# Eleven modulation units move from the context's chain into the first block's chain

## The chip, the cores and the metric

The kernel runs on one core of a Trainium2 chip. The metric is the device time of one execution in microseconds (us); several runs are given by their median. A core has a matrix engine (PE, with PEld as its weight loads), a vector engine (DVE), a scalar engine (ACT), a general engine (POOL) and a sync engine (SP), each with an instruction stream of its own, and 16 transfer engines (DMA) that move data between the chip's memory and the core's buffers. Here all large loads are issued from SP, in one order.

## The reference

Two networks follow each other on 256 tokens of width 1024. The first is one block: gated attention in two branches, a cross attention, and a mixture of 32 experts of which every token uses two. The second has two layers on the tokens `h` and on a context `hc` of 256 rows. Both streams are modulated by vectors that come from `c` and `c_ctx`:

```
def first_block(x, ...):
    merged = (sigmoid(gate_a) * (y_a @ w_branch_a) + sigmoid(gate_b) * (y_b @ w_branch_b))
    x = x + merged @ w_out
    x = x + cross_attention(rms_norm(x), rms_norm(mem), w_cq, w_ckv, w_co)
    return x + hier_moe(rms_norm(x), ..., w_exp_gate, w_exp_up, w_exp_down)

def second_block(x, c, ctx, c_ctx, ...):
    for layer in range(2):
        mod  = (silu(c)     @ ada_w[layer] + ada_b[layer])   # 9 vectors of 1024
        modc = (silu(c_ctx) @ ada_w[layer] + ada_b[layer])
        h  = h  + 0.5 * mod[2]  * swiglu(modulate(h,  mod[0],  mod[1]),  ...)
        hc = hc + 0.5 * modc[2] * swiglu(modulate(hc, modc[0], modc[1]), ...)
        yx, yc = mixer(modulate(h, mod[3], mod[4]), modulate(hc, modc[3], modc[4]))
        h = h + mod[5] * yx
        h = h + 0.5 * mod[8] * swiglu(modulate(h, mod[6], mod[7]), ...)
        # the same for hc, in the first layer
```

A modulation unit, in what follows, is one of the nine vectors of one layer, for both streams at once: a product of two columns with a 1024 x 1024 part of `ada_w`, which is 4 MB. There are eighteen. The context's chain through the second network needs nothing of the first: it needs `ctx`, the modulation and the weights alone.

## The kernel before

The program is written as two streams, each a `Stream` with its own buffers. **fore** (tiles whose names begin with f) runs the first network (`first_block`, `moe`) and then the tokens of the second network (`tokens()`). **back** (names with b) runs the context's chain (`context()`). Loads of fore are 1 MB and go through a ring of four buffers (`raw`, shown as fraw); those of back are 0.5 MB, with a ring of five (braw). Every instruction of a stream follows the one before it on the same engine (`Kern.link`), so a stream's order is the order in which it is written. Between the two streams a scheduler chooses by priorities: `SEG` gives each part of the program a start and a slope, and the priority grows with the matmul work that the stream has issued. The first block and the routing start at -5000, so they come first where they can, and back fills in; the expert part starts at 365, among the context's parts c0a (300), c0b (530), c0c (680).

A weight that is loaded is split into a high and a low part (ACT writes sph, DVE for fore and POOL for back write spl), and each product is three matmuls of 128x256. Two kinds of load are used without a split: the experts' weights (in_w_eg, in_w_eu, in_w_ed; 128x512 matmuls on 32 columns of weights) and `ada_w` (128x256 matmuls against the two columns of `scol`, written into fps or bps).

The stages in time are these. The first block: projections, attention, then eight passes of gates (`branch_gates(n)` with two loads' worth of w_g and half a load of w_br), four passes of the output projection (`out_proj`), a query projection, the cross attention, and the routing. Then the expert loads, in eight groups of 24 loads of 1 MB (16 up and gate, 8 down). Then a loop for further blocks of the routing, which has no pass here; it splits the program, and everything of `context()` must stand ahead of it. Last the tokens, with the rest of the context's work (`late`, by the table `PLAN`: 'r' is a step of the context's third feed-forward part, 'a' a modulation unit, 'k' keys and values for the odd mixer).

The modulation units before: twelve at the head of `context()` (all nine of layer 0, three of layer 1), by `Kern.ada` in loads of 0.5 MB that take turns in the tags raw, k4, xh and xl of back; two in the token stage ('aa' in `PLAN[8]`); four in the odd mixer, by `ada_wide`. `ada_close` ends each with a transpose and an addition on DVE. The first feed-forward part of the context (c0a) needs units 0 to 2 of layer 0, its even mixer (c0b) units 3 to 5, and so on.

Of the kernel before, what the change touches and what calls it, by code (L numbers as in the profile page):

```python
# [20 lines left out]
KC = 8  # L21
# [9 lines left out]
ADA_TAGS = ('raw', 'k4', 'raw', 'xh', 'k4', 'raw', 'xl', 'k4', 'raw')  # L31
# [71 lines left out]
class Ahead:  # L103
# [7 lines left out]
    def step(self, c):  # L111
        K, S, nc = self.K, self.S, self.K.nc
        if self.X is None:
            xh, xl = (S.t(tag, [128, KC, T + 2], F32R) for tag in ("xh", "xl"))
            s = self.shift[:, :, None].to_broadcast([128, KC, 2])
            nc.scalar.activation(xh[:, :, T:], s, AF.Copy)
            nc.vector.tensor_tensor(xl[:, :, T:], s, xh[:, :, T:].bitcast(F32), op=OP.subtract)
            self.X = X2([xh[:, k] for k in range(KC)], [xl[:, k] for k in range(KC)])
        K.split_to(self.X.h[c][:, :T], self.X.l[c][:, :T], self.res[c], self.g[:, c:c + 1])
# [29 lines left out]
class Kern:  # L149
# [209 lines left out]
    def out_proj(self, S, src, X, res, gate, step=None):  # L359

        nc = self.nc
        for u in range(4):
            raw = self.pair(S, src[u])
            p = S.ps([128, 2, T])
            for i in range(2):
                self.proj_f(S, raw[i], KC, X, p[:, i])
            if gate is None:
                nc.vector.tensor_tensor(res[:, 2 * u:2 * u + 2], res[:, 2 * u:2 * u + 2], p, op=OP.add)
            else:
                self.update(res, p, gate, 2 * u)  # L370
            if step:
                step(2 * u)
                step(2 * u + 1)
            self.squares(S, res, 2 * u)

    def update(self, res, p, gate, d):
# [173 lines left out]
    def ada_wide(self, S, l, ms):  # L550

        for m in ms:
            p = S.ps([128, 512])
            for u in range(KC // 2):
                raw = self.load(S, self.I["ada_w"][l, m, u])
                for i in range(2):
                    k = 2 * u + i
                    mv = raw[:, i * 1024:(i + 1) * 1024].rearrange("p (c j i) -> p j c i", j=4, i=32)
                    for j in range(4):
                        self.mm(p[32 * j:32 * j + 32, 0:256], self.sc[:, k], mv[:, j], k == 0, k == KC - 1)  # L560
                if u < KC // 2 - 1:
                    yield
            self.ada_close(S, l, m, p)
            yield

    def ada_close(self, S, l, m, p):
        nc = self.nc
# [142 lines left out]
    def first_block(self, S):  # L710
# [66 lines left out]
        p = S.ps([128, 512])  # L777
# [9 lines left out]
        raw = self.pair(S, I["w_ck"])  # L787
        p = S.ps([128, 2, T])
# [87 lines left out]
        for i in range(8):  # L876
# [7 lines left out]
            if i < 6:  # L884
                p = queries(i + 2)
# [15 lines left out]
        def branch_gates(n):  # L901
            p = S.ps([128, 2, T])
            ts = []
            raw = self.pair(S, I["w_g"][n])
            for s in range(2):
                self.proj_f(S, raw[s], KC, X, p[:, s])
            for s in range(2):
                t = S.t("k1", [128, T])
                nc.scalar.activation(t, p[:, s], AF.Tanh, scale=0.5)
                ts.append(t)  # L910
            return ts
# [10 lines left out]
        XB = X2([ybh[:, i] for i in range(4)], [ybl[:, i] for i in range(4)])  # L922
        mg = [S.t("k4", [128, 4, T]) for _ in range(2)]
        for n in range(8):
            ts = ahead if n == 0 else branch_gates(n)
            if n % 2 == 0:
                rb = self.load(S, I["w_br"][n // 2])
            p = S.ps([128, 2, T])
            o = (n % 2) * 1024
            self.proj_f(S, rb[:, o:o + 512], 4, XA, p[:, 0])  # L930
            self.proj_f(S, rb[:, o + 512:o + 1024], 4, XB, p[:, 1])
            for s in range(2):
                nc.vector.scalar_tensor_tensor(ts[s], ts[s], 1.0, p[:, s], op0=OP.add, op1=OP.mult)
            nc.vector.tensor_tensor(mg[n // 4][:, n % 4], ts[0], ts[1], op=OP.add)
# [7 lines left out]
        raw = self.pair(S, I["w_cq"])  # L942
        q = S.t("k2", [128, 2, T])
        p = S.ps([128, 2, T])
        for n in range(2):
            self.proj_f(S, raw[n], KC, X, p[:, n])
        nc.scalar.activation(q, p, AF.Copy, scale=0.125)
        rx = self.rstd_cols(S, self.stats(S, chunks))
        yy = S.t("k4", [128, 2, 2, T], F32R)
        ps = {}  # L950

# [8 lines left out]
        for c in range(2):  # L960
            Ps, r = self.softmax(S, pp[2 * c:2 * c + 2], (T, T), rx)
            for s in range(2):
                self.scaled(Ps[s], r[:, s], (T, T))
                ps[c, s] = Ps[s]
        for c in range(2):
            PT = S.t("k4", [128, 2, 2, T])
            for s in range(2):
                pt = S.ps([128, 2, 2, 128])
                for b in range(2):
                    for kb in range(2):  # L970
                        nc.tensor.transpose(pt[:, kb, b], ps[c, s][:, b, kb * 128:(kb + 1) * 128], ident)
                if s == 0:
                    nc.vector.tensor_copy(PT[:, s], pt.rearrange("p k b q -> p k (b q)"))
                else:
                    nc.scalar.activation(PT[:, s], pt.rearrange("p k b q -> p k (b q)"), AF.Copy)
            po = S.ps([128, 512])
            for kb in range(2):
                for s, rows in enumerate(HALVES):
                    hv = slice(64 * (2 * c + s), 64 * (2 * c + s) + 64)
                    self.mm(po[rows, :T], vc[:, kb, hv], PT[:, s, kb, :], kb == 0, kb == 1)  # L980
            self.split_to(yy[:, c, 0], yy[:, c, 1], po[:, :T])
        Y = X2([yy[:, 0, 0], yy[:, 1, 0]], [yy[:, 0, 1], yy[:, 1, 1]])
        raw = self.load(S, I["w_co"])
# [16 lines left out]
    def moe(self, S):  # L1000
# [3 lines left out]
        st = self.stats(S, None)  # L1004
        rx = self.rstd_cols(S, st)
        lg = self.token_major(S, 36, 2, ((self.w_route, keep),))

        xh, xl = S.t("xh", [128, 2, 1024], F32R), S.t("xl", [128, 2, 1024], F32R)
        hm = [(xh[:, b], xl[:, b]) for b in range(2)]

        def turn(b, a):
            pt = S.ps([128, 512])
            for i in range(4):
                nc.tensor.transpose(pt[:, i * 128:(i + 1) * 128], keep[4 * a + i][:, b * 128:(b + 1) * 128],
                                    self.ident)
            self.split_to(hm[b][0][:, a * 512:(a + 1) * 512], hm[b][1][:, a * 512:(a + 1) * 512], pt, rx[:, b:b + 1])
# [4 lines left out]
        def ct(n):  # L1021
            used[0] += n
            return scratch[:, used[0] - n:used[0]]
# [24 lines left out]
        tt(dg, G, gm[:, :, None].to_broadcast([128, 2, 4]), op=OP.subtract)  # L1048
        nc.scalar.activation(dg, dg, AF.Exp)
        turn(0, 0)  # L1050
        gw = S.t("c", [128, 2])
        red(gw, dg, axis=AX.X, op=OP.add)
        nc.vector.reciprocal(gw, gw)
# [10 lines left out]
        tt(e2, t2, t1, op=OP.subtract)  # L1064
        nc.scalar.activation(e2, e2, AF.Exp)
        turn(0, 1)
        ts(r, e2, 1.0, None, op0=OP.add)
        nc.vector.reciprocal(r, r)
        tt(w[:, 0], r, gw, op=OP.mult)
# [12 lines left out]
        self.mm(p[:, 64:96], self.ones, A[:, 1], False, True)  # L1082
        turn(1, 0)
        turn(1, 1)
        cnt, nsp, inc, sb = ct(32), ct(32), ct(32), ct(32)
        rank = ct(64).rearrange("p (b n) -> p b n", b=2)
        nc.vector.tensor_copy(rank, p[:, :64].rearrange("p (b n) -> p b n", b=2))
# [705 lines left out]

SPILL = 4
DEFER = 0
PLAN = {-1: 'rrr', 0: 'r', 6: 'r', 8: 'raak'}
PLAN_N = 32
CUT = ((0, 9, 9, 9, 9), (0, 3, 3, 3, 3))
FORE = dict(raw=4, sph=3, spl=3, xh=1, xl=1, k1=6, k2=4, k4=6, c=16, q1=4, dg=2, ld=1, dst=6, wg=2, gc=5, c72=1, rope=1)
BACK = dict(raw=5, sph=3, spl=3, xh=1, xl=1, k1=4, k2=4, k4=3, c=16, q1=2, wg=1, gc=4, c72=1)  # L1800
SEG = dict(c1b=(1150, 2), first=(-5000, 1), ada=(0, 0), c0a=(300, 1.25), c0b=(530, 1.3), c0c=(680, 1.3), ada1=(950, 3), c1a=(1050, 4.8),
# [4 lines left out]
def kernel(ctx: ExitStack, tc: tile.TileContext, I, out, dbg=None, stop=None):  # L1806
# [7 lines left out]
    def context():  # L1814
        c = K.cres
        back.seg(*SEG["ada"])
        def ada(part):
            for l in range(2):
                ms = range(CUT[l][part], CUT[l][part + 1])
                for _ in K.ada(back, l, ms, ADA_TAGS if part == 0 else ("raw",)):  # L1820
                    pass
        K.adapart = ada
        ada(0)
        back.seg(*SEG["c0a"])
        X = K.modulated(back, c, 0, 0, 1)
        K.ffn(back, c, X, 0, 0, K.mods_col(0, 2, 1))
        if dbg:
            dbg("hc0a", c)
        ada(1)
        back.seg(*SEG["c0b"])  # L1830
        X = K.modulated(back, c, 0, 3, 1)
        K.even(back, c, X, K.mods_col(0, 5, 1), 1)
        if dbg:
            dbg("hc0b", c)
        ada(2)
        back.seg(*SEG["c0c"])
        X = K.modulated(back, c, 0, 6, 1)
        K.ffn(back, c, X, 0, 1, K.mods_col(0, 8, 1))
        ada(3)
        back.seg(*SEG["c1a"])  # L1840
        X = K.modulated(back, c, 1, 0, 1)
        K.c1a = K.ffn_steps(back, c, X, 1, 0, K.mods_col(1, 2, 1))
        K.nada = CUT[1][-1]
        late(PLAN.get(-1, ""))
        if dbg:
            dbg("hc0c", c)
# [50 lines left out]
            dbg("h1c", x)  # L1897

    K.cur, K.stream = back.chain, back
    if stop != "first0":  # L1900
        context()
    K.cur, K.stream = fore.chain, fore
    fore.seg(*SEG["first"])
    K.first_block(fore)
    if stop in ("first", "first0"):
        return
    fore.seg(*SEG["route"])
    K.moe(fore)
    if stop == "moe":
        return  # L1910
    steps = tokens()
# [167 lines left out]
```

## Time and profile before

| what | value |
|---|---|
| median of 3 runs | 2572.41 us (2569.87 to 2574.41) |
| profiled run, its own time | 2570.27 us |
| its span in the profile | 2568.5 us |
| mean granted clock of PE | 0.967 |
| PE busy | 2379.0 us, 93% |
| bytes moved | 617.37 MB |

Durations below come from the profiled run; the span runs from its first to its last recorded instruction. Busy time is a mean over stages with different limits, so the rows are given by stages: the opening (0 to 64 us), two stretches with the modulation's loads (64 to 211), gates, output projection and query (211 to 370), cross attention and routing (370 to 448), the expert loads (448 to 1319) and the tokens. PEclk is the granted clock of PE as a share of full speed; the DMA share is the mean over the core's 16 transfer engines.

### The profile page before, as it was taken

The numbers are of one execution on the slowest core, as the hardware profiler recorded it, in microseconds if no ns is written. First come the engines' busy times: TensorE is split into PE (matmuls) and PEld (weight loads), VectorE is DVE, ScalarE is ACT, GpSimd is POOL, SyncE is SP. The second block draws the span as 40 slices with busy tenths as digits, with TensorE's granted clock in tenths as the row PEclk, the third lists the DMA queues.
The fourth block names the chain that finished last, engine by engine and source line by source line (L and its number), as shares of the span: only waits on it lengthen the run. The fifth ranks groups of instructions, "written<-read, shape, count | busy, mean of one in ns | idle before, by whom it ended". The sixth has DMA issues, their size and how long they took to land. (4 is left out here: it accounts for less than half of the span.)

```text
span 2568.5 us, 48423 instructions
## 1 busy us (share of the span) xinstructions
PE 2379.0 (93%) x19032; PEld 2065.5 (80%) x19032; DVE 1481.0 (58%) x3179; ACT 1186.0 (46%) x2342; POOL 729.7 (28%) x584
## 2 busy tenths in 40 slices
PE   6999998998988999999579999999999899899998
PEld 4767998885666887877259998878999899767998
DVE  6546667325444333252157676657767766677766
ACT  4434554344433433443035555545555555465554
POOL 1001245663425665756041004231000100424000
PEclk9999998999989999999889999999999999899998
DMA  9896543997979997988874554462455455355552
GB/s 376 307 343 252 186 158 115 387 355 287 379 285 358 353 352 297 363 328 334 337 295 174 183 182 139 166 208 106 154 191 181 148 182 186 109 197 197 180 182 99
DMA packets 115238, 617.37 MB, mean 240 GB/s; under 512 B 13232, under 2 KB 14704, under 8 KB 63936
## 3 DMA queue, kind: packets, MB, share of 16 engines
q1 hardware_dynamic: 113616, 610.20, 64.4%
q0 software_dynamic: 1392, 4.06, 0.5%
q8 instruction: 150, 2.46, 0.4%
q14 instruction: 80, 0.66, 0.1%
HBM read 612.11 MB, written 2.10 MB: 239 GB/s over the span
## 5 line engine op out<-in xcount | busy, mean ns | idle before, releaser
L58 POOL TENSOR_TENSOR bspl<-braw,bsph 128x512 fp32r<-128x512 f32 x468 | 608.2, 1308 | 894.7 <-ACT bsph L58 759.2
L58 ACT ACTIVATE fsph<-fraw 128x512 fp32r<-128x512 f32 x764 | 478.5, 628 | 516.7 <-PE fps L58 432.8
L58 DVE TENSOR_TENSOR fspl<-fraw,fsph 128x512 fp32r<-128x512 f32 x712 | 501.1, 707 | 286.2 <-ACT fsph L58 281.2
L58 PE MATMUL fps<-fxh,fspl 128*128 128x256 f32 (+1 forms) x2000 | 572.5, 286 | 5.0 <-POOL fspl L58 2.5
L58 PE MATMUL fps<-fxh,fsph 128*128 128x256 f32 (+1 forms) x2000 | 573.3, 287 | 3.0 <-ACT fxh L58 2.4
L58 PE MATMUL fps<-fxl,fsph 128*128 128x256 f32 (+1 forms) x2000 | 568.6, 284 | 6.4 <-DVE fxl L58 6.4
L58 ACT ACTIVATE bsph<-braw 128x512 fp32r<-128x512 f32 x468 | 291.0, 629 | 394.8 <-PE bps L58 325.4
L58 PEld LDWEIGHTS fps<-fxl,fsph 128*128 128x128 f32 x2000 | 382.3, 191 | 9.8 <-DVE fxl L58 9.1
L58 PEld LDWEIGHTS fps<-fxh,fspl 128*128 128x128 f32 x2000 | 381.2, 191 | 11.1 <-DVE fspl L58 5.3
L58 PEld LDWEIGHTS fps<-fxh,fsph 128*128 128x128 f32 x2000 | 382.7, 191 | 9.2 <-ACT fxh L58 4.1
L58 PE MATMUL bps<-bxh,bsph 128*128 128x256 f32 x1264 | 364.3, 288 | 6.1 <-ACT bsph L58 4.3
L58 PE MATMUL bps<-bxh,bspl 128*128 128x256 f32 x1264 | 364.5, 288 | 3.9 <-POOL bspl L58 3.7
L58 PE MATMUL bps<-bxl,bsph 128*128 128x256 f32 x1264 | 361.3, 286 | 2.6 <-ACT fk L58 2.2
L58 PE MATMUL fps<-fk,fsph 128*128 128x256 f32 x1632 | 298.7, 284 | 1.8 <-ACT fk L58 1.1
L58 PEld LDWEIGHTS bps<-bxh,bsph 128*128 128x128 f32 x1264 | 244.2, 193 | 29.6 <-issue 11.9
L58 PEld LDWEIGHTS bps<-bxh,bspl 128*128 128x128 f32 x1264 | 244.0, 193 | 24.1 <-POOL bspl L58 16.8
L58 PEld LDWEIGHTS fps<-fk,fsph 128*128 128x128 f32 x1632 | 254.8, 192 | 5.6 <-ACT fk L58 2.3
L58 PEld LDWEIGHTS bps<-bxl,bsph 128*128 128x128 f32 x1264 | 244.3, 193 | 10.8 <-issue 8.1
L58 PE MATMUL fps<-fraw,fk 128*32 128x512 f32 (+1 forms) x1600 | 211.6, 643 | 33.2 <-DMA fraw<-in_w_eu_dram 19.9
L58 POOL TENSOR_TENSOR fk<-fk,fk 128x512 f32<-128x512 f32 x16 | 21.2, 1322 | 774.0 <-ACT fk L58 768.9
L58 PE MATMUL fps<-fk,fspl 128*128 128x256 f32 x816 | 230.8, 283 | 0.0
L58 DVE SCALAR_TENSOR_TENSOR bk<-bk,bps 128x256 f32<-128x256 f32 (+1 forms) x148 | 60.4, 412 | 249.1 <-ACT bk L58 247.2
(359 smaller groups left out, 3477.9 us busy)
## 6 DMA issues: line engine op xcount, KB each, us to landing
fraw<-in_ffn_in_dram SPq DMA_DIRECT2D x88, 1024.0 KB, 4.9
braw<-in_ffn_in_dram SPq DMA_DIRECT2D x132, 512.0 KB, 6.5
fraw<-in_w_eg_dram SPq DMA_DIRECT2D x66, 1024.0 KB, 7.3
fraw<-in_w_eu_dram SPq DMA_DIRECT2D x66, 1024.0 KB, 9.2
fraw<-in_w_ed_dram SPq DMA_DIRECT2D x66, 1024.0 KB, 7.1
fraw<-in_ffn_out_dram SPq DMA_DIRECT2D x44, 1024.0 KB, 4.9
braw<-in_ffn_out_dram SPq DMA_DIRECT2D x66, 512.0 KB, 6.3
braw<-in_ada_w_dram SPq DMA_DIRECT2D x59, 512.0 KB, 7.8
```

The lines of the kernel that those rows point to most:

```text
L58: r = f(*args, **kw)
```

## The change

The head of `context()` keeps three units (0 to 2 of layer 0). Eleven others (3 to 8 of layer 0, 0 to 4 of layer 1) are now written into the fore stream, by a generator `ada_mix` that loads two times 1 MB in a step and uses them at once; a unit is two steps. `mixed(place)` runs the steps that the table `MIX` names: one ahead of each of the eight gate passes, one in each of the four output passes, and ten more from the query projection to the ranks of the routing. `context()` is a generator: what follows c0a is recorded inside `moe`, after the last step, since it needs these units. The two units of the token stage are among the eleven, and `PLAN[8]` loses its 'aa'. The four in the odd mixer stay.

```diff
@@ out_proj
                 step(2 * u + 1)
+                self.mixed("out")
@@ Kern
+    def ada_mix(self, S, units):
+        for l, m in units:
+            p = S.ps([128, 512])
+            for u in range(0, KC // 2, 2):
+                raws = [self.load(S, self.I["ada_w"][l, m, u + i]) for i in range(2)]
+                for i in (1, 0):
+                    for a in range(2):
+                        mv = raws[i][:, a * 1024:(a + 1) * 1024].rearrange("p (c j i) -> p j c i", j=4, i=32)
+                        for j in range(4):
+                            self.mm(p[32 * j:32 * j + 32, 0:256], self.sc[:, 2 * (u + i) + a], mv[:, j],
+                                    u == 0 and i == 1 and a == 0, u > 0 and i == 0 and a == 1)
+                if u == 0:
+                    yield
+            self.ada_close(S, l, m, p)
+            yield
+
+    def mixed(self, place):
+        for _ in range(MIX.get(place, 0)):
+            next(self.mix)
@@ first_block
         for n in range(8):
+            self.mixed("gates")
             ts = ahead if n == 0 else branch_gates(n)
...
+        self.mixed("query")
...
         for c in range(2):
+            self.mixed("flip")
@@ moe
         lg = self.token_major(S, 36, 2, ((self.w_route, keep),))
+        self.mixed("route")
...
         turn(0, 0)
+        self.mixed("first")
...
         turn(0, 1)
+        self.mixed("second")
...
         turn(1, 1)
+        self.mixed("rank")
+        assert next(self.mix, None) is None
+        yield
@@
-PLAN = {-1: 'rrr', 0: 'r', 6: 'r', 8: 'raak'}
+PLAN = {-1: 'rrr', 0: 'r', 6: 'r', 8: 'rk'}
-CUT = ((0, 9, 9, 9, 9), (0, 3, 3, 3, 3))
+MIX_UNITS = [(0, m) for m in range(3, 9)] + [(1, m) for m in range(5)]
+MIX = dict(gates=1, out=1, query=2, flip=1, route=1, first=1, second=2, rank=2)
@@ context
-        ada(0)
+        for _ in K.ada(back, 0, range(3), ADA_TAGS):
+            pass
         back.seg(*SEG["c0a"])
...
+        yield
         back.seg(*SEG["c0b"])
...
-        K.nada = CUT[1][-1]
+        K.nada = 5
@@ driver
-        context()
+    ctx_steps = context()
+    next(ctx_steps)
...
+    K.mix = K.ada_mix(fore, MIX_UNITS)
     K.first_block(fore)
...
-    K.moe(fore)
+    moe = K.moe(fore)
+    next(moe)
+    K.cur, K.stream = back.chain, back
+    assert next(ctx_steps, None) is None
+    K.cur, K.stream = fore.chain, fore
+    assert next(moe, None) is None
```

The order on SP around the second load of w_g, before (128x2048 is 1 MB, 128x1024 is 0.5 MB; braw, bk, bxh and bxl are back's buffers):

```order
L58 DMA fraw_10665<-in_w_g_dram 128x2048
L58 DMA bk_620<-in_ada_w_dram 128x1024
L58 DMA braw_630<-in_ada_w_dram 128x1024
L58 DMA bxh_632<-in_ada_w_dram 128x1024
L58 DMA bk_642<-in_ada_w_dram 128x1024
L58 DMA braw_644<-in_ada_w_dram 128x1024
L58 DMA bxl_654<-in_ada_w_dram 128x1024
```

The same place on SP after, in the gates:

```order
L58 DMA fraw_4820<-in_w_g_dram 128x2048
L58 DMA fraw_4890<-in_w_br_dram 128x2048
L58 DMA fraw_4928<-in_ada_w_dram 128x2048
L58 DMA fraw_4930<-in_ada_w_dram 128x2048
L58 DMA braw_1617<-in_ffn_in_dram 128x1024
L58 DMA fraw_4953<-in_w_g_dram 128x2048
L58 DMA fraw_5060<-in_ada_w_dram 128x2048
L58 DMA fraw_5062<-in_ada_w_dram 128x2048
```

The loads of `ada_w` stood one after another in back's several buffers, and the gates' own loads between them; now they alternate with the gates' loads in the one ring fraw, and back's loads there are weights of the context's feed-forward part.

On PE, at the start of a gate pass, before (fps is an accumulator of fore; fxh and fxl are the high and low parts of the block's input):

```order
L58 MATMUL fps_11167<-fk_10603,fsph_11184 128x256
L58 MATMUL fps_11167<-fk_10602,fspl_11185 128x256
L58 MATMUL fps_11203<-fxh_9080,fsph_11206 128x256
L58 MATMUL fps_11203<-fxl_9081,fsph_11206 128x256
L58 MATMUL fps_11203<-fxh_9080,fspl_11207 128x256
```

At the start of such a pass on PE after:

```order
L58 MATMUL fps_5283<-fk_4586,fsph_5300 128x256
L58 MATMUL fps_5283<-fk_4585,fspl_5301 128x256
L58 MATMUL fps_5319<-fraw_5322,scol 32x256 x8
L58 MATMUL fps_5319<-fraw_5320,scol 32x256 x8
L58 MATMUL fps_5340<-fxh_3063,fsph_5343 128x256
L58 MATMUL fps_5340<-fxl_3064,fsph_5343 128x256
L58 MATMUL bps_1512<-bk_1311,bsph_1508 128x256
```

A step of sixteen matmuls on two 1 MB loads stands ahead of the pass, and matmuls of the context's feed-forward part (bps) stand inside it.

On SP near the end of the expert loads, before, the last load of the context's chain stands in the seventh group, among its down weights (in_w_ed):

```order
L58 DMA braw_8796<-in_ffn_out_dram 128x1024
L58 DMA braw_8868<-in_ffn_out_dram 128x1024
L58 DMA braw_8870<-in_ffn_out_dram 128x1024
L58 DMA fraw_13922<-in_w_ed_dram 128x2048
L58 DMA fraw_13924<-in_w_ed_dram 128x2048
L58 DMA fraw_13934<-in_w_ed_dram 128x2048
```

After, it stands ahead of that group's first load:

```order
L58 DMA braw_12029<-in_ffn_out_dram 128x1024
L58 DMA braw_12101<-in_ffn_out_dram 128x1024
L58 DMA braw_12103<-in_ffn_out_dram 128x1024
L58 DMA fraw_13817<-in_w_eg_dram 128x2048
L58 DMA fraw_13819<-in_w_eu_dram 128x2048
L58 DMA fraw_13829<-in_w_eg_dram 128x2048
```

The context's chain ends some sixteen expert loads earlier in the order.

## Rows read from the trace of the kernel before

**Rows 1.** The page's shares: engine, busy us, share of the span, instructions.

```profile
PE 2379.0 (93%) x19032; PEld 2065.5 (80%) x19032; DVE 1481.0 (58%) x3179; ACT 1186.0 (46%) x2342; POOL 729.7 (28%) x584
```

**Rows 2.** Windows: length; busy PE, PEld, DVE, ACT, POOL; PEclk, DMA share, GB/s.

```profile
0.00:64.00 64.00, 41.27 (x323) 29.70 (x323) 43.03 (x134) 29.16 (x62) 7.80 (x18) 0.97 0.98 376
64.00:141.00 77.00, 73.61 (x703) 57.58 (x703) 42.85 (x111) 30.03 (x79) 0.00 (x0) 0.98 0.86 315
141.00:211.00 70.00, 64.00 (x565) 39.70 (x563) 31.69 (x87) 21.43 (x58) 0.00 (x0) 1.00 0.94 357
211.00:370.00 159.00, 154.78 (x1281) 147.72 (x1280) 109.61 (x224) 87.81 (x184) 39.75 (x31) 1.00 0.51 178
370.00:448.00 78.00, 70.89 (x530) 66.49 (x530) 56.67 (x127) 37.19 (x76) 44.74 (x35) 0.91 0.38 123
448.00:552.00 104.00, 104.00 (x864) 85.69 (x860) 31.95 (x61) 41.22 (x75) 68.06 (x54) 1.00 0.97 374
552.00:838.00 286.00, 256.42 (x1866) 188.47 (x1859) 129.08 (x334) 115.50 (x234) 125.34 (x101) 0.93 0.85 326
838.00:1226.00 388.00, 380.10 (x3074) 312.75 (x3073) 140.71 (x274) 154.29 (x287) 245.47 (x190) 0.99 0.90 339
1226.00:1319.00 93.00, 54.07 (x337) 19.52 (x336) 12.15 (x25) 8.81 (x15) 7.55 (x6) 0.82 0.89 334
1319.00:2568.00 1249.00, 1179.90 (x9512) 1117.87 (x9512) 883.22 (x1805) 660.53 (x1277) 190.94 (x152) 0.97 0.48 169
```

**Rows 3.** A window of the token stage in which PE is dense.

```profile
1412.00:1541.00 129.00, 129.00 (x1091) 129.00 (x1091) 90.19 (x168) 67.81 (x122) 0.00 (x0) 1.00 0.52 184
```

**Rows 4.** Groups by shape, whole span: modulation from 1 MB loads (busy, mean ns, idle).

```profile
L58 PE MATMUL fps<-fraw,scol 128*32 128x256 f32 x256 | 17.1, 385 | 0.0
```

**Rows 5.** Window 64 to 211, modulation alone; one of three 512-column groups there.

```profile
64.00:211.00 147.00, 45.91 (x592) 18.24 (x592) 0.00 (x0) 0.99 0.90 335
...
L58 PE MATMUL fps<-fsph,fxh 128*128 128x512 f32 x16 | 6.8, 423 | 0.0
```

**Rows 6.** Waits of PE, 64 to 211 us: total us, times, longest.

```profile
PE fps L58 <- DVE fq L58: 3.8, 3, 2.1
PE fps L58 <- DVE fk L58: 2.5, 1, 2.5
...
PE fps L58 <- ACT fq L58: 1.3, 1, 1.3
```

**Rows 7.** The window with expert loads and no filler (30 loads).

```profile
1226.00:1307.00 81.00, 44.77 (x264) 10.63 (x263) 7.92 (x18) 3.20 (x6) 0.03 (x1) 0.79 0.93 355
```

**Rows 8.** Waits of PE, 1226 to 1319 us.

```profile
PE fps L58 <- DMA fraw<-in_w_eu_dram: 19.9, 7, 4.5
PE fps L58 <- DMA fraw<-in_w_ed_dram: 12.2, 4, 4.9
```

**Rows 9.** Timeline of PE: the first expert matmuls, of four loads (start, duration).

```profile
447.58 3.64 PE L58 MATMUL fps<-fraw,fk 128*32 128x512 f32 x32
```

**Rows 10.** Waits of PE, 552 to 838 us, the two largest.

```profile
PE bps L58 <- DVE bk L58: 13.8, 10, 2.9
PE bps L58 <- ACT bk L58: 11.7, 10, 3.0
```

**Rows 11.** Waits of SP's queue, 448 to 1226 us, the largest.

```profile
SPq L58 <- POOL bspl L58: 369.3, 132, 10.2
```

**Rows 12.** Token stage: PE's wait in 1641 to 1740 us; two windows of it.

```profile
PE bps L58 <- DMA braw<-in_ada_w_dram: 6.1, 2, 3.4
...
1701.00:1717.00 16.00, 16.00 (x144) 12.20 (x136) 6.37 (x17) 7.22 (x14) 0.56 (x1) 1.00 0.84 268
1717.00:1733.00 16.00, 9.95 (x97) 6.49 (x86) 7.03 (x15) 3.46 (x7) 3.46 (x3) 0.79 0.84 288
```

**Rows 13.** Transfer issues on SP: count, KB each, median us from issue to landing.

```profile
fraw<-in_ada_w_dram SPq DMA_DIRECT2D x16, 1024.0 KB, 4.9
fraw<-in_w_g_dram SPq DMA_DIRECT2D x8, 1024.0 KB, 4.9
```

More of the change, by code (lines that the diff above doesn't have):

```diff
@@ L1816, in context @@
         back.seg(*SEG["ada"])
[L1817 to L1822, printed above, removed]
-        ada(0)
+        for _ in K.ada(back, 0, range(3), ADA_TAGS):
+            pass
         back.seg(*SEG["c0a"])
@@ L1828, in context @@
             dbg("hc0a", c)
-        ada(1)
+        yield
         back.seg(*SEG["c0b"])
@@ L1834, in context @@
             dbg("hc0b", c)
-        ada(2)
         back.seg(*SEG["c0c"])
@@ L1838, in context @@
         K.ffn(back, c, X, 0, 1, K.mods_col(0, 8, 1))
-        ada(3)
         back.seg(*SEG["c1a"])
@@ L1899 @@
     K.cur, K.stream = back.chain, back
-    if stop != "first0":
-        context()
+    ctx_steps = context()
+    next(ctx_steps)
     K.cur, K.stream = fore.chain, fore
     fore.seg(*SEG["first"])
+    K.mix = K.ada_mix(fore, MIX_UNITS)
     K.first_block(fore)
```

## Prediction

> **What bounds the kernel now.** I read the shares of the page first [rows 1]: the matrix engine (PE) is busy for 2379 of 2568.5 us. So the whole run is nearly a sum of PE work, and a change that only moves PE work can win or lose only in the 190 us in which PE stands idle, or where it is slowed. The windows by stage [rows 2] show where those are. The opening (0 to 64 us) has loads at 0.98 of the transfer engines. From 64 to 211 us the modulation loads run at 0.86 and 0.94. From 211 to 448 us (gates, output projection, query, routing) PE is nearly full and the transfer engines are at 0.51 and 0.38. From 448 to 1319 us run the expert loads, at 0.85 to 0.97, with the context's matmuls as filler beside them; this ends in a stretch without filler (1226 to 1319 us) in which PE is busy for 54 of 93 us at a granted clock of 0.82. The rest, 1249 us, is the token stage, PE-bound. The first expert matmul stands at 447.58 us [rows 9].
>
> So two stretches are short of transfer time (64 to 211, and 448 to 1319), one lies between them that has it to spare, and the end of the expert stage is short of PE work. The change takes modulation loads out of the first and puts them into the spare stretch. But the context's other work comes forward with it.
>
> **Stage 1, up to the first expert matmul.** The orders show what stands ahead of that matmul on PE. Context matmuls of 256 columns: 713 before, 1431 after, so 718 more, since the chain has no longer twelve units to wait for but three. One costs 0.118 us where PE is dense (1091 instructions in 129 us, [rows 3]): 718 × 0.118 = **+85 us**, on the path, as PE is what sets this stage. Modulation units ahead of it: 12 before, 14 after, the two extra ones from the token stage. The four units that the token stage runs from 1 MB loads take 17.1 us in 256 instructions [rows 4], 4.3 us each: **+8.6 us**.
>
> What is won: from 64 to 211 us PE's own work comes to 592 modulation instructions × 0.067 (17.1 us ÷ 256) = 39.7 us, 48 instructions of 512 columns (three rows of 16, of which one stands in [rows 5]; 0.23 us each beside two of 256) = 11 us, and the other 628 of the 1268 × 0.118 = 74 us: 125 of 147 us. So 22 us are lost there, while loads run near full. After, 36 MB of the modulation's loads have left this stretch. Waits for the block's own vector work stay: 3.8 + 2.5 + 1.3 us [rows 6]. I take **−15 us**, between −22 (all of it) and −8.
>
> What is paid: the 22 steps fetch 44 loads of 1 MB through the fore stream's ring of four, in turn with w_g, w_br and w_out, and a load lands 4.9 us after its issue [rows 13]. In the SP queue after, two of the gates' eight passes need 2 w_g, 1 w_br and 4 modulation loads and about 1 MB of the context's: 8 MB beside some 25 us of PE work (17.0 + 4.3 + about 3.5 us, counted as above), 320 GB/s. The row from 448 to 552 us moves 374 GB/s [rows 2], so the rate suffices; what may not suffice is the distance by which the ring of four runs ahead. Counted in the orders at the prices above, a fore load in gates and output projection had 17 to 40 us of PE work between its issue and its use before; it has 7 to 14 us after. The nearest row is the expert stage from 838 to 1226 us: the same ring of four, 339 GB/s, and PE idle for 7.9 of 388 us. For about 220 us of such steps that makes 4.5 us; with the vector engines' splits in between I double it: **+9 us**, from 0 to +60. The upper end is each step showing one landing less its matmuls, 22 × (4.9 − 2.15).
>
> Routing (370 to 448 us) has 7.1 idle us [rows 2], with steps and context matmuls now queued in it; 0 to −5, taken as 0. The six extra ada_close on the fore chain are two vector instructions each at places where PE works on; nothing. Stage 1: 447.6 + 85 + 8.6 − 15 + 9 = **535 us**.
>
> **Stage 2, the expert loads, 447.6 to 1319.3 us (871.7 us).** What came forward is missing here: 718 matmuls. In the orders the context's last chained matmul stands ahead of expert load 146 of 192 now, ahead of load 162 before; so 46 loads instead of 30 run with no filler. In the trace the 30 took 81 us (1226 to 1307), 2.7 us each, at 355 GB/s and a granted clock of 0.79 [rows 7], with PE waiting for up and down weights 19.9 + 12.2 us in the 93 us [rows 8]. Sixteen more at 2.8 us: the stretch grows from 93 to **138 us**.
>
> The part with filler (448 to 1226 us, 778 us) loses 85 us of filler, and 16 loads' own PE work (3.64 us for 4 loads [rows 9], 14.6 us): if PE sets it, 778 − 99 = 679. If transfers set it: bytes issued between the routing's list and the end of the stage fall from 292.6 to 276.9 MB in the orders; less 1 MB for each load without filler, 262.6 and 230.9 MB, and at the rate of before (262.6 MB in 778 us, 337 GB/s) 684 us. Both rules agree, because both engines were nearly full; I take **678**. Against a faster one stands the context's even mixer: from 552 to 838 us PE waits for its vector work (13.8 + 11.7 us, [rows 10]) and no row there names a transfer; that chain stays whole and only moves earlier, into groups 0 to 2. On SP the largest wait is for the context's splits on POOL (369 us, [rows 11]), and both streams' loads queue behind it; it keeps. Stage 2: 678 + 138 = **816 us**, 56 less.
>
> **Stage 3, the tokens, 1249 us.** Two units leave: 2 × 4.3 = 8.6 us of PE; the two waits for their loads, 6.1 us, and 16 us at a granted clock of 0.79 around them [rows 12] leave too: −8.6 to −22, taken **−14**. What was late behind them is the context's next step, which now stands a little earlier.
>
> **The sum.** 535 + 816 + 1235 = 2586 us against 2568.5; with the 1.8 us by which the profiled run lies above its span, 2588. That run is 2.1 us under the median of 2572.41, so half of that is added: **2589 us**, 0.7% slower. In one sentence: the change wins about 15 us where loads were short and 14 us among the tokens, and pays some 31 us more than it gains for moving filler from the expert loads, which leave PE idle, to the first block, which doesn't.
>
> **Rivals.** *(A) Transfers set the expert stage, and fewer bytes and less PE work end it earlier: faster.* For it: transfer shares of 0.97, 0.85 and 0.90 [rows 2], and a stretch at 374 GB/s where PE was full too. PE's own work with filler is 778 − 38 idle = 740, less 99 = 641 us; the tail 46 × 2.7 = 124: at the very best 765 us. With +72 in stage 1 and −20 in stage 3 that would be 2515. Half of the way there from my own sum, with stage 1 at +78, stage 2 at 790 (−82) and stage 3 at −16: 2570 + 78 − 82 − 16 = **2550 us**. Against it: the waits in 552 to 838 us are not for transfers. It decides if the part with filler runs at 355 GB/s or more instead of 337.
>
> The Trainium skill's page "DMA: Bandwidth & Descriptors" (Specifications) gives about 358 GB/s as the limit of one core; by it the 276.9 MB would need 773 us at least, and the best of (A) would be 2523 us. The 374 GB/s of the row are above that figure, so by this trace it is no limit, and no number here uses it.
>
> *(B) The ring of four shows its loads at most steps: clearly slower.* Three quarters of the upper end above, +45 us instead of +9, and nothing given back later, as the token stage starts when the expert stage ends: 2589 + 36 = **2625 us**. For it: two consecutive 1 MB loads per step, in the only ring that w_g also uses, and a lookahead of 7 us at the shortest against 4.9 us to landing plus a split. Against it: the same ring feeds the experts with hardly a wait.
>
> *(C) It cancels.* The stage that loses its filler is helped by as much as stage 1 pays (stage 2 at 800 instead of 816): **2573 us**, within 0.2%.
>
> **How the numbers follow.** My forecast, slower by 6 to 40 us, has 0.45; (A) 0.25; (B) 0.15; (C) 0.15. About 5 us, 0.2%, is what a measurement of this kernel can tell from no change. Faster 0.25, same 0.15, slower 0.60. The range takes in most of (A) and of (B): 2542 to 2632 us; the forecast's own is 2578 to 2612.
>
> **What would show it.** The first expert matmul at 525 to 550 us; at 560 or more (B) is right, and PE's waits between 211 us and it will name modulation or w_g loads. The stretch 64 to 211 us with hardly a modulation load and PE full. The expert stage 800 to 830 us long with PE waiting for expert loads over its last 46; under 790, with over 350 GB/s ahead of that stretch, (A). The token stage 1227 to 1241 us. The forecast fails if the context's extra matmuls stand ahead of the first expert matmul in gaps that PE had anyway, since the 85 us are priced as dense work.

## The result, and the profile after

The changed kernel takes 2588.69 us (median of 7 runs, 2583.34 to 2592.09), the kernel before 2573.78 us beside it: a ratio of 1.0057, with a 95% interval of 1.0044 to 1.0069. It is slower by 15 us. Its profiled run has a span of 2586.9 us, 18.4 more than that of before.

The windows by stage of the changed kernel (columns as in [rows 2]; the stages begin at the same places of the program: opening, attention, gates to query, cross attention and routing, expert loads with filler, expert loads without, tokens):

```profile
0.00:64.40 64.40, 41.78 (x322) 30.07 (x323) 42.96 (x133) 29.03 (x61) 7.80 (x18) 0.97 0.97 373
64.40:144.50 80.10, 77.84 (x642) 69.23 (x641) 55.09 (x140) 44.75 (x111) 15.23 (x12) 0.96 0.46 160
144.50:228.20 83.70, 83.27 (x645) 78.42 (x643) 50.45 (x105) 44.80 (x101) 44.85 (x34) 1.00 0.47 156
228.20:428.60 200.40, 197.40 (x1874) 177.38 (x1873) 109.90 (x223) 89.73 (x185) 57.30 (x43) 1.00 0.83 305
428.60:517.90 89.30, 84.88 (x764) 75.10 (x765) 56.52 (x136) 38.88 (x76) 48.66 (x38) 0.96 0.71 272
517.90:614.00 96.10, 87.20 (x623) 61.49 (x622) 51.19 (x119) 38.87 (x77) 42.67 (x35) 0.93 0.91 343
614.00:900.00 286.00, 264.81 (x2000) 204.78 (x2000) 107.14 (x273) 114.42 (x226) 140.26 (x112) 0.95 0.88 338
900.00:1196.00 296.00, 289.49 (x2309) 235.37 (x2311) 104.85 (x218) 115.91 (x213) 178.81 (x139) 0.98 0.88 336
...
1340.00:2586.00 1246.00, 1175.22 (x9384) 1118.04 (x9384) 880.77 (x1800) 660.47 (x1276) 191.90 (x152) 0.97 0.46 163
```

Compare with [rows 2]: in the attention the transfer share fell from 0.86 and 0.94 to 0.46 and 0.47, and PE is nearly full (161 of 164 us); from there to the experts it rose from 0.51 and 0.38 to 0.83 and 0.71. The modulation's loads are where the change puts them. The first expert matmul, beside [rows 9], and the stretch of expert loads without filler, beside [rows 7]:

```profile
517.86 3.64 PE L58 MATMUL fps<-fraw,fk 128*32 128x512 f32 x32
...
1199.00:1340.00 141.00, 81.36 (x468) 24.22 (x466) 15.55 (x35) 10.35 (x18) 7.63 (x6) 0.73 0.93 354
```

The waits of PE there (1196 to 1340 us, beside [rows 8]), from 64 to 518 us the one that names a modulation load, with the largest, and from 518 to 1196 us the two of the even mixer (beside [rows 10]):

```profile
PE fps L58 <- DMA fraw<-in_w_eu_dram: 35.5, 14, 4.7
PE fps L58 <- DMA fraw<-in_w_ed_dram: 14.9, 5, 5.5
...
PE fps L58 <- DVE fc L58: 3.8, 1, 3.8
PE fps L58 <- DMA fraw<-in_ada_w_dram: 1.4, 2, 0.8
...
PE bps L58 <- DVE bk L58: 12.8, 11, 3.3
PE bps L58 <- ACT bk L58: 9.6, 11, 3.0
```

| stage | before | forecast | after | moved |
|---|---|---|---|---|
| to the first expert matmul | 447.6 | 535 | 517.9 | +70.3 |
| experts with filler | 778 | 678 | 681 | -97 |
| experts without filler | 93 | 138 | 141 | +48 |
| tokens | 1249.2 | 1235 | 1246.8 | -2.4 |
| span | 2568.5 | 2586 | 2586.9 | +18.4 |

The sum came out as forecast. Two of its terms did not: stage 1 grew by 70 instead of 88 us, and the tokens gave 2 instead of 14. The experiments ask whether the reason given, moved filler (context work that PE does beside other waits), is what costs the 15 us.

All ratios below are to the kernel before on the same chip, with 95% intervals. Single runs of one kernel spread by 8 to 19 us. The kernel before and four later variants have the same program up to the first expert matmul, and it stands at 447.6 to 453.1 us in their five profiles; so I take stage lengths from two single profiles as told apart by about 5 us and not less.

### The profile page after: what moved, and what is told of

It reads as the page before. It is cut to its first block, busy times and chain, and to the rows that moved or that the text cites. A ratio compares the mean times of both kernels' runs of the same rounds, so it can differ in the third digit from the quotient of the medians.

```text
span 2586.9 us, 48344 instructions
## 1 busy us (share of the span) xinstructions
PE 2386.3 (92%) x19032; PEld 2075.6 (80%) x19032; DVE 1474.4 (57%) x3179; ACT 1187.2 (46%) x2342; POOL 735.1 (28%) x584
## 5 line engine op out<-in xcount | busy, mean ns | idle before, releaser
L58 PEld LDWEIGHTS bps<-bxh,bsph 128*128 128x128 f32 x1264 | 246.3, 195 | 30.2 <-issue 12.9
L58 PE MATMUL fps<-fraw,fk 128*32 128x512 f32 (+1 forms) x1600 | 221.9, 672 | 52.6 <-DMA fraw<-in_w_eu_dram 35.5
L58 PE MATMUL bps<-bk,bsph 128*128 128x256 f32 x1056 | 199.4, 286 | 1.3 <-ACT bk L58 1.2
```

What stands on the lines that cost most here:

```text
L58: r = f(*args, **kw)
```

## Is it the context's early start? Two runs that hold it back

Theory 1 was the prediction's sentence: what costs is that filler leaves the expert loads for the first block. Theory 2 was that the steps cost by their place. The edit leaves the steps where they are, and ties the start of the context's feed-forward part to the PE instruction that ends step 4, or step 12:

```diff
         for _ in range(MIX.get(place, 0)):
             next(self.mix)
+            self.nmix += 1
+            if self.nmix == CTX_AT:        # 4, or 12
+                self.start_ctx()
...
+    def start_ctx():
+        K.after["tensor"] = fore.chain["tensor"]
+        K.cur, K.stream = back.chain, back
+        next(ctx_steps)
+        K.cur, K.stream = fore.chain, fore
```

> The changed kernel, but the context's first feed-forward part may start on PE only behind the fourth of the 22 modulation steps. The steps stay where the change put them. Context matmuls ahead of the first expert matmul fall from 1431 to 675 (713 in the kernel before), and the context's chain ends some 16 to 20 expert loads before the end instead of 46. Theory 1 (the change pays for the filler that it takes from the end of the expert stage, and the steps themselves cost only their PE work): the first expert matmul at 425 to 445 us instead of 518, the expert stage 840 to 860 us instead of 822, the whole 2540 to 2560 us, faster than both kernels. Theory 2 (the steps cost, by their place in the first block's chain and in its ring of four loads, whatever the context does): the first expert matmul not under 460 us, the whole 2570 us or more.

> As the run before, with the start of the context's chain behind the twelfth step: 459 context matmuls ahead of the experts, and filler for all but some 8 expert loads. Theory 1: the tail without filler shrinks further, by some 10 loads at 1.8 us of idle PE each, but the first block has less to fill its own waits; the whole 2530 to 2560 us. Theory 2: 2570 us or more, as PE then waits for the steps' loads with nothing beside them.

Measured: step 4, 1.0075 (1.0058 to 1.0092), 2593.19 us; step 12, 1.0113 (1.0095 to 1.0131), 2605.02 us. Neither is faster than the changed kernel, and the second is slower. Theory 1 falls, and theory 2's bound for the first expert matmul holds (471.4 us, not under 460). Where the filler's return went is seen in the windows of the first of the two: the attention, and the tail, which now has 24 loads without filler instead of 46. Under them are its four largest waits of PE from 64 to 195 us.

```profile
64.50:194.60 130.10, 107.06 (x743) 90.85 (x741) 71.79 (x179) 54.69 (x144) 3.77 (x3) 0.87 0.32 117
1263.00:1343.00 80.00, 47.84 (x293) 18.77 (x291) 10.96 (x23) 7.97 (x14) 7.62 (x6) 0.77 0.86 328
...
PE fps L58 <- DVE fq L58: 8.3, 4, 2.1
PE fps L58 <- ACT fq L58: 5.6, 2, 4.6
PE fps L58 <- DVE fk L58: 4.7, 2, 4.2
PE fps L58 <- ACT fk L58: 3.8, 5, 0.8
```

With hardly any filler (one modulation unit) the attention still takes 130 us, for 90 us of PE work by the orders: the block waits for its own vector and scalar work (22.4 us by these four rows), and the granted clock falls to 0.87. Filled with 125 us of work, as before, it took 147 us; with 154 us, as after, 163.8. So filler costs about half its work there: (163.8 - 130.1) / (154 - 90) = 0.53. Over the whole of stage 1, holding back 756 matmuls (89 us) gave 517.9 - 471.4 = 46.5 us. From there on this kernel takes 2586.9 - 471.4 = 2115.5 us against 2069.0, 46.5 us more. In these two profiles the filler's move between the two stages is neutral, with half the work hidden at either place; by the medians it is neutral or a little worse to move it back (0.18%, with an interval of -0.03 to 0.39).

Beside the kernel before, this run shows what is still paid when the context's filler is back. Its attention is 17 us shorter (130.1 against 147.3), for 35 us less work. From the gates to the first expert matmul it is 40.5 us longer (276.8 against 236.3), for some 41 us more work by the same prices (44 of modulation more, 3 of context less). The modulation thus left a stretch that hid half of it for one that here hides none. In the changed kernel, with more context work there too, that second stretch grew by 53.5 us for 64.

## Do the steps cost by themselves? The same steps in the attention

```diff
+            self.mixed("attn")              # in each of the eight attention passes
...
+            if n < 6:
                 self.mixed("gates")
-MIX = dict(gates=1, out=1, query=2, flip=1, route=1, first=1, second=2, rank=2)
+CTX_AT = 16
+MIX = dict(attn=2, gates=1)
```

> The changed kernel's steps, but sixteen of the 22 stand in the attention of the first block (two in each of its eight passes, 64 to about 210 us) and six in the first six gate passes; the context's chain may start on PE behind the sixteenth. Context matmuls ahead of the experts: 711, as in the kernel before (713); units ahead of them: 14. Theory 3, formed on the last runs (a stretch charges for added PE work what its gaps leave: about half in the attention, where the block waits for its own vector work, all of it from the gates on): 34 us of steps move from full price to half, 2593 - 17 = 2576 us, between 2568 and 2582. Rival (the steps cost by being in the first block's chain and its ring of four loads, wherever they stand): 2588 us or more.

Measured: 1.0129 (1.009 to 1.0169), 2608.42 us. The theory formed on the last two runs (theory 3: half price in the attention, so 2576) fails, and the rival's bound holds. The first expert matmul stands at 492.03 us, 44 us later than in the kernel before, with two units (8.6 us) more ahead of it. The waits of PE and those of SP's queue, both from 64 to 250 us:

```profile
PE fps L58 <- DMA fraw<-in_ada_w_dram: 16.2, 9, 4.2
...
SPq L58 <- DVE fspl L58: 89.9, 10, 13.0
SPq L58 <- PE fps L58: 38.7, 32, 3.4
SPq L58 <- DMA fraw<-in_ada_w_dram: 17.2, 9, 4.0
```

Here the ring of four shows: SP stands for 90 us, in ten waits, each time ahead of a modulation load whose slot is freed only when DVE has split the weight that held it; PE then waits nine times for a modulation load. In the changed kernel the same steps wait 1.4 us in all. So rival (B) is a real mechanism, at a place where the ring's other loads are split late, and not in the gates. In the kernel before, SP waits for the same splits there, ahead of fore's own weights, and PE hardly waits for a modulation load (both rows from 64 to 211 us):

```profile
SPq L58 <- DVE fspl L58: 45.8, 9, 7.7
...
PE bps L58 <- DMA bk<-in_ada_w_dram: 1.8, 2, 1.2
```

Its modulation loads use back's buffers under four tags. That this is what keeps them in time is likely, and no run here separates it.

## Which of the moved units cost? Nine, six, and two elsewhere

Three kernels move fewer units, or the same number to another place. Nine ran first; head5 and six were designed on its result.

```diff
 # nine: two units stay in the token stage, the last four steps fall away
-PLAN = {-1: 'rrr', 0: 'r', 6: 'r', 8: 'rk'}
+PLAN = {-1: 'rrr', 0: 'r', 6: 'r', 8: 'raak'}
-MIX_UNITS = [(0, m) for m in range(3, 9)] + [(1, m) for m in range(5)]
+MIX_UNITS = [(0, m) for m in range(3, 9)] + [(1, m) for m in range(3)]
-MIX = dict(gates=1, out=1, query=2, flip=1, route=1, first=1, second=2, rank=2)
+MIX = dict(gates=1, out=1, query=2, flip=1, route=1, first=1, second=0, rank=0)
 # head5: as nine, but PLAN[8] is 'rk' and the two stand at the head of context()
+        for l, ms in ((0, range(3)), (1, range(3, 5))):
+            for _ in K.ada(back, l, ms, ADA_TAGS):
 # six: as nine, but units 0 to 2 of layer 1 stand at the head of context()
+MIX = dict(gates=1, out=1)
```

> The changed kernel with nine units in the steps; the other two stay in the token stage as in the kernel before ('aa'), and the last four steps, in the routing, fall away. Theory 3: 8.6 us of PE leave the routing at nearly full price, and the token stage takes them for the 2.4 us that it gave when they left: 2588.7 - 6 = 2582 us. Rival (the prediction's price of 14 us in the token stage): 2594 us.

> Nine units in steps as in the nine-unit kernel (none of the last four steps in the routing), and the two units of the token stage at the head of the context's chain: eleven moved, as in the changed kernel, but the last two to another place. Theory R (the steps in the routing are what costs, since the ranks and the expert list wait behind them): 2575 to 2580 us, as nine. Theory T (what costs is that these two units leave the token stage, which gives only 2.4 us for them): 2583 to 2589 us, as the changed kernel.

> Six units in twelve steps (gates and output projection only); three units of layer 1 stand at the head of the context's chain again, beside units 0 to 2 of layer 0; two stay in the token stage. Context matmuls ahead of the experts: 1239. Against the nine-unit kernel, 12.9 us of PE work go from the query projection and the routing, where PE is dense, to the attention. Theory 3 (half price there): 6 us faster than nine, about 2571 us. Rival (the context's matmuls fill those gaps already, so full price there too): within 2 us of nine, 2576 to 2580 us.

| kernel | ratio | interval | median us |
|---|---|---|---|
| changed, eleven | 1.0057 | 1.0044 to 1.0069 | 2588.69 |
| nine | 1.0017 | 1.0001 to 1.0034 | 2577.68 |
| head5 | 1.0046 | 1.003 to 1.0061 | 2585.66 |
| six | 1.0067 | 1.0051 to 1.0082 | 2590.8 |

Nine is 0.40% below the changed kernel (half-widths of 0.125 and 0.165 points, together 0.21): 10 us, 5 to 16. That is under both numbers expected for it (2582 and 2594). So a third to all of the 15 us belongs to the two units of the token stage and their four steps. The token stage gave little for them: from the end of the last expert matmul it takes 1255.5 to 1264.5 us in the five profiles that have lost them (mean 1259.3: changed, late4, late12, attn, head5) and 1259.6 to 1262.0 us in the three that have them (mean 1261.1: before, nine, six). Two windows of the changed kernel at the place where those units stood, and the largest waits of PE from 1708 to 1780 us, beside [rows 12]:

```profile
1727.00:1744.00 17.00, 14.36 (x85) 12.41 (x84) 15.03 (x38) 9.85 (x21) 1.87 (x2) 0.80 0.18 62
1744.00:1774.00 30.00, 26.64 (x204) 26.16 (x203) 13.20 (x39) 15.79 (x33) 5.92 (x6) 0.91 0.13 47
...
PE fps L58 <- ACT fk L58: 2.7, 1, 2.7
PE bps L58 <- ACT bxh L58: 1.5, 1, 1.5
PE fps L58 <- DVE fk L58: 1.2, 2, 0.7
PE bps L58 <- DVE bxl L58: 1.1, 4, 0.5
```

The waits for their loads are gone, and PE waits there for the normalised context (bxh, bxl) and for results of ACT and DVE (fk) instead: from 1727 to 1774 us PE is idle for 6.0 of 47 us, and its clock is at 0.80 and 0.91. That the units had covered these waits is argued from their place. Matched by the program's order, the fore stream was 4.9 us ahead of where the kernel before would put it (a lag of 16.4 us against 21.25 at the stage's start) when it came to this place, and 0.3 us behind that (21.5) at its end; the lag then stays near 18.6.

Head5 was to tell the place from the leaving: against nine it is 0.29% slower (7.5 us; 0.06 to 0.52%), against the changed kernel 0.11% faster, within the intervals. This is where theory T put it (2583 to 2589), and it fits the token stage, which gave back some 2 of the two units' 8.6 us. Whether they then stand in the routing or at the head is not resolved. A rival stays open: a unit may cost by standing at the head, since six, which has three more there than nine, is slower than nine too.

Six goes against theory 3 again, and against its rival (2576 to 2580). It takes 12.9 us of units out of the query projection and the routing, and is 0.50% slower than nine (0.27 to 0.73%). Its first expert matmul stands 3.1 us later than nine's (505.5 against 502.42 us), with 12.5 us less PE work ahead of it by the orders; from there to the end of the last expert matmul it takes 823 us against 805, and has those 12.5 us more to do. Beside nine's routing stretch stand the same of the changed kernel (shown above) and of the kernel before; all begin at the first use of w_co and end at the first expert matmul. Nine's, then that of before, then that of tailb2, a kernel of the next section whose program is that of before up to the expert loads:

```profile
429.20:502.40 73.20, 67.44 (x562) 62.07 (x560) 56.48 (x128) 34.56 (x69) 41.64 (x33) 0.98 0.56 197
...
370.20:447.60 77.40, 70.29 (x527) 66.33 (x526) 56.56 (x127) 36.87 (x75) 44.14 (x35) 0.91 0.38 123
374.60:448.40 73.80, 66.41 (x524) 63.20 (x522) 55.19 (x125) 35.97 (x74) 45.48 (x34) 0.98 0.40 129
```

Nine has more instructions in this stretch than before (562 against 527), a granted clock of 0.98 instead of 0.91, and is 4.2 us shorter; PE idles in it for 5.8 us against 7.1. But tailb2 runs the instructions of before in the same order, and has a clock of 0.98 and 73.8 us. So two executions of the same code differ by as much, and the 4.2 us can't be put down to the steps. The changed kernel's stretch is 16 us longer than nine's, for four steps (8.6 us) and 70 context matmuls (8.3 us): there added work was paid in full. The 0.50% between six and nine has several parts and its cause was not separated further.

## Filling the tail from the token stage

These edits change only the table `PLAN`: one or both early steps of the context's third feed-forward part move from the token stage to the end of the expert loads.

```diff
-PLAN = {-1: 'rrr', 0: 'r', 6: 'r', 8: ...}
+PLAN = {-1: 'rrrrr', 8: ...}        # tail, tailb, tailb5, sixtail
+PLAN = {-1: 'rrrr', 6: 'r', 8: ...} # tailb1
+PLAN = {-1: 'rrrr', 0: 'r', 8: ...} # tailb2
```

> The changed kernel with two more steps of the context's third feed-forward part ahead of the loop, taken from the token stage (PLAN -1 'rrrrr' instead of 'rrr', none at 0 and 6): 518 more context matmuls beside the expert loads, filler up to about load 174 of 192 instead of 146. Theory 1 (PE stands idle in the tail and 61 us of work fit there): the token stage loses some 61 us, the expert stage gains 20 to 35, the whole 2550 to 2565 us. Rival (the tail is bound by transfers, and the 10 MB that come with the work cost as much there as PE saves): expert stage longer by 50 or more, the whole 2575 to 2590 us.

> The kernel before with the same two steps moved ahead of the loop; modulation as it was. Filler then lasts to about load 190 of 192. Theory 1: the idle 39 us of the tail are filled, the whole 2535 to 2555 us, so that the kernel before gains about as much by this as the changed one loses. Rival (transfers): 2565 to 2580 us.

> The kernel before with one step of the context's third feed-forward part (288 matmuls, 34 us of PE, 6 MB) moved from the start of the token stage ahead of the loop (PLAN -1 'rrrr', 6 'r'). With both steps moved the stage of the experts grew by 41 us and the token stage shrank by 44, for 61 us of PE work each. Theory 3: the first step finds the larger gaps of the tail, so one step gains more than half of the two: 2562 to 2569 us. Rival (the gain of the two is by the second): 2570 to 2576 us.

> As the run before, but the step that is moved is the one at place 6 of the token stage, and the one at its start stays (PLAN -1 'rrrr', 0 'r'). Theory 3: the same price in the expert stage; what the token stage gives back depends on the waits that the step covered there, and place 6 stands in the feed-forward part, where PE is dense (dense price 34 us), place 0 at its start: 5 to 15 us faster than the run before, 2552 to 2562 us. Rival (both places cover waits alike): within 3 us of the run before.

> The six-unit kernel with both early steps of the context's third feed-forward part ahead of the loop (PLAN -1 'rrrrr', none at 0 and 6). In the kernel before this gained 8 us, in the changed kernel 2. If the gaps at the end of the expert stage decide, which are between those two here (some 40 loads without filler against 30 and 46): 3 to 8 us faster than six, 2563 to 2570 us. Rival (the token stage pays for what it loses): within 2 us of six.

> The kernel before with both steps moved ahead of the loop, a second time, since one step alone was slower than none and the 8 us of gain were from one chip: if the gain is the kernel's, 2562 to 2569 us again; if it was that chip's, 2572 us or more.

| kernel | ratio | interval | median us |
|---|---|---|---|
| changed + both (tail) | 1.0047 | 1.003 to 1.0064 | 2586.54 |
| before + both (tailb) | 0.9972 | 0.9957 to 0.9987 | 2565.77 |
| before + both, second time (tailb5) | 0.9974 | 0.9962 to 0.9986 | 2565.69 |
| before + the one at 0 (tailb1) | 1.0034 | 1.0017 to 1.0051 | 2582.92 |
| before + the one at 6 (tailb2) | 1.0015 | 1.0002 to 1.0028 | 2580.63 |
| six + both (sixtail) | 1.0044 | 1.003 to 1.0058 | 2584.63 |

In the changed kernel 61 us of work (518 matmuls) went beside the expert loads; its expert stage grew by 38 us and its token stage shrank by 38, so neither theory's price held; the time lies where the rival put it, and against the changed kernel nothing is resolved. In the kernel before, moving both steps gains 0.26 to 0.28%, twice, on two chips: 6 to 8 us, at the rival's end of what was expected the first time and as expected the second. One step alone loses, which neither theory expected: both theories of tailb1 had it at 2576 us or less. And tailb2 is within 3 us of tailb1, as its rival said (0.19%, with an interval of -0.02 to 0.40). The waits of PE for DVE in the token stage point to why, the largest row each: of the kernel before, with one step moved (tailb1), and with both (tailb5).

```profile
PE fps L58 <- DVE fk L58: 29.5, 17, 3.7
...
PE fps L58 <- DVE fk L58: 46.7, 17, 6.0
...
PE fps L58 <- DVE fk L58: 48.3, 20, 6.0
```

The first step that leaves uncovers 17 us of waits, the second almost none. So one step, 34 us of PE work in tailb1 and 27 in tailb2, takes some 13 us off the token stage (from the end of the last expert matmul 1262 us before, 1248 with one, 1215 with both) and adds 18 to 20 to the experts; the second step takes off 33 more and adds 23 to 26. In tailb5 the windows of the expert loads and of the tail are these:

```profile
448.00:1323.00 875.00, 834.18 (x6546) 662.70 (x6546) 325.45 (x715) 348.74 (x662) 502.43 (x393) 0.97 0.90 341
1323.00:1361.00 38.00, 19.30 (x112) 6.41 (x110) 10.43 (x22) 5.60 (x11) 2.56 (x2) 0.74 0.67 258
```

Ten expert loads are left without filler. This kernel is faster than both, without any of the change. With six it gains too (0.23%, 0.02 to 0.44, against six), as expected in size, but doesn't reach the kernel before.

## Why the prediction was right, and where it wasn't

**The total**: 2589 us forecast, 2588.69 measured. That it is met within 1 us is luck, by errors that cancel: stage 1 came out 17 us shorter than forecast (517.9 against 535), the expert stage 6 us longer and the tokens 12 us longer.

**Stage 1, +88 forecast, +70.3 measured.** The step that failed is the pricing of 718 matmuls and two units as dense work with +9 for the ring. By the orders 93 us of PE work were added, and the attention took 29 of them in 17 us (147 to 164), which is the -15 of the sum within 3 us. The rest, 64 us from the gates to the experts, took 53.5. The ring's +9 was not paid: 1.4 us of waits name a modulation load. And the gaps of gates and routing, priced at nothing to -5, hid some 11. The prediction named this, matmuls in gaps that PE had anyway, as what would make it fail.

**Why the attention had 22 us to win.** I read the 22 us as loads that run late. The trace of before already spoke against it: PE waits 1.8 us for a modulation load there. The run that holds the context back showed another reading: that stretch takes 130 us with hardly anything to fill it, so most of its gap is the block's own vector work and the lower clock, and the modulation was its filler. The size was right and the mechanism was not.

**Stage 2, -56 forecast, -49.5 measured.** The part with filler 681 against 678; sixteen more loads without filler at 2.8 us, 141 against 138 us. Both rules that agreed on 679 and 684 held, and nothing here tells them apart. The even mixer's waits stayed (12.8 + 9.6 us against 13.8 + 11.7), as did the transfer rate (336 to 343 GB/s with filler).

**Stage 3, -14 forecast, -2.4 measured.** The step that failed is that the units' PE work, "the two waits for their loads, 6.1 us, and 16 us at a granted clock of 0.79 around them [rows 12] leave too": waits for vector and scalar results and a clock of 0.80 stood at that place afterwards, and not even the 8.6 us of PE work came back. The prediction named the context's next step behind the units and gave it no price. Nine puts 5 to 16 of the 15 us on these two units, with what they cost at the new place.

**The reason in one sentence**, filler moved from the expert loads to the first block, fell with the run that undoes it: the two stages hide about the same share of the context's work. What that run still pays stands ahead of the experts, where the modulation left the attention for the gates and the routing. Theory 3, built on such stage lengths, failed in both of its direct tests: in attn PE waited for the steps' loads instead, and in six the cause is open. What is left after the two units, 0.17% (0.01 to 0.34), is small, and the experiments don't split it.

**Rivals.** (A) needed 355 GB/s with filler; the rate stayed at 336 to 343. (B) needed waits for the steps' loads; there were 1.4 us, and only at another place, in the attention, did it come true. (C) was off by the 15 us that the stage sums show.

## To carry to other kernels

An idle gap is not a stock that any added work can draw from: before a unit is moved, ask at both places what the work hides, since a filler that leaves uncovers the wait behind it. Price moved filler by the length of the same stretch with less and with more of it, not by the dense duration of an instruction; here a profile without filler would have given the 0.53 at once. And steps that share a small ring cost little only where the ring's other loads are released in time (1.4 us of waits in the gates here, 16.2 in the attention).

## What was not expected of the hardware

In the attention the granted clock was 0.96 to 1.00 with filler and 0.87 with hardly any (late4, late12), where PE stood idle for 23 of 130 us. By the page "TensorE: Matmul & The Clock Gate" of the Trainium skill (Part 1), the engine's default is the throttled state and activity releases it; these rows agree. So a part of what filler hides there may be the block's matmuls at the higher level; that part was not separated from the hidden waits. The clock alone is no sign of filler, though: with the same instructions, the routing had 0.91 before, in tailb1 and in tailb5, and 0.98 in tailb2, 73.8 us against 77.4 to 78.2.
